# Norm rows spread by products with ones, and four places for rectified index scores

## The chip, the cores and the metric

The kernel runs on one core of one Trainium2 chip. The metric is the device time of one execution in microseconds (us). TensorE is called PE here, VectorE DVE, ScalarE ACT, GpSimd POOL and SyncE SP, as in the profile.

## The reference

A trunk of two layers for 1024 tokens of width 1024. Layer 0 mixes tokens with a gated short convolution, layer 1 with sparse attention: an indexer scores all earlier keys, the best 256 are kept, and attention runs over them. Each mixer and each mixture of experts is followed by a residual sum and a layer norm.

```python
for i in range(DEPTH):                       # 2 layers
    m = short_conv_mixer(x, ...) if i % 2 == 0 else dsa_mixer(x, ...)
    x = layer_norm(DEEPNORM_ALPHA * x + m, ln1_g[i], ln1_b[i])
    f = hier_moe(x, router_wg[i], ..., exp_w1[i], exp_w3[i], exp_w2[i])
    x = layer_norm(DEEPNORM_ALPHA * x + f, ln2_g[i], ln2_b[i])     # the second norm

def layer_norm(x, g, b):
    y = (x - mu) * rsqrt(var + LN_EPS) * g + b       # g and b: one row of 1024 for all tokens

# in dsa_mixer, for each block of 128 queries and 8 indexer heads of 64
s_idx = einsum('bthd,bsd->bths', q_idx, k_idx) * 64 ** -0.5
score = einsum('bths,bth->bts', relu(s_idx), w_idx)
```

The mixture has 8 groups of 8 experts of hidden width 256 (SwiGLU), two experts of one group for each token.

## The kernel before, in words

All work is written out in program order; each engine takes its own instructions in that order. SBUF holds an arena of 26 slots of 128 x 2048 f32. `take()` gives the slot that was freed longest ago, `give()` puts slots at the end of the list. An instruction that writes a slot waits until the last reader of its earlier contents is done.

`moe(l, ...)` goes over 32 pairs of experts, four pairs to a group of experts. For pair `p` it runs `up(p)` on PE (the products with both experts' first and third matrices, line 870, 64 instructions in column halves), `act(p)` (lines 878, 879), the sums of the pair before (`add`, line 922), `turn(p)` (line 885), at the last pair of a group `select()` for the next group (line 855), and `down(p)` (line 896). `down` makes two halves of 128 x 512; each half is read from PSUM by ACT (line 900), by DVE (line 901) and, up to pair 27, by ACT again (line 903). `select`, `turn` and `down` take their PSUM tiles in turn from the pool `psr`, which has three buffers; `up` has a buffer of its own. The expert matrices, 1 MB each, are loaded by SP (line 792) as soon as slots are free: `prefetch` is called behind every `give`. A pair uses six of them. `gather` and `scatter` on POOL bring and write rows of tokens; `finish` applies the second norm to a group's rows and first runs behind `down(4)`. Behind pair 6 `count_over` reads a number into registers, and the engines wait for it.

The second norm's scale and shift are needed in all 128 partitions. `load_ln` takes a slot behind pair 2 and loads each of the two rows with a DMA on ACT's queue that reads the same row for every partition (lines 161, 162).

In `attention()`, `index_queries(g)` makes the queries of two indexer heads on PE (lines 222 to 224, called `mm3`), ACT and DVE split them (1378, 1380), and SP swaps partition halves through `tm` (1383, 1384). One group later `scores(g)` is woven into the next `index_queries`: ACT first writes the swapped halves (1388, 1389); then, for each head and each of six blocks of queries, PE makes the scores in a PSUM tile of two banks (1401, 1402, pool `psL`, two buffers), ACT rectifies them into `r` (1405), and DVE adds `r` times the head's weight to the block's sum (1408 for the first head, 1410 for the others). `r` alternates between the two halves of one slot, `rl`. POOL splits the weights of the attention queries beside this (1423, 1424). The attention queries of 16 heads follow on PE, beside the search for the best keys on ACT and DVE.

Of the kernel before, what the change touches and what calls it, by code (L numbers as in the profile page):

```python
# [23 lines left out]
F32 = mybir.dt.float32  # L24
# [4 lines left out]
AF = mybir.ActivationFunctionType  # L29
# [4 lines left out]
P = 128  # L34
T = 1024
D = 1024
# [30 lines left out]
class Net:  # L67
# [32 lines left out]
    def constants(self):  # L100
        nc, c = self.nc, self.const
        sl = self.take()
        jp = self.slots[sl].bitcast(I32)[:, :P]
        nc.gpsimd.iota(jp, pattern=[[1, P]], base=0, channel_multiplier=-1)
        self.ident = c.tile([P, P], F32, name="ident")
        nc.vector.tensor_scalar(self.ident, jp, 0.0, None, op0=OP.is_equal)
        self.tri = c.tile([P, P], BF16, name="tri")
        nc.vector.tensor_scalar(self.tri, jp, 0.0, None, op0=OP.is_gt)
        self.ones = c.tile([P, P], BF16, name="ones")
        nc.vector.memset(self.ones, 1.0)  # L110
        self.io64 = c.tile([P, NE], F32, name="io64")
        nc.gpsimd.iota(self.io64, pattern=[[1, NE]], base=0, channel_multiplier=0,
                       allow_small_or_imprecise_dtypes=True)
        self.ioP = c.tile([P, NE], F32, name="ioP")
        nc.gpsimd.iota(self.ioP.rearrange("p (a b) -> p a b", a=2), pattern=[[1, 2], [2, NP]],
                       base=0, channel_multiplier=0, allow_small_or_imprecise_dtypes=True)
        self.tcol = c.tile([P, 1], F32, name="tcol")
        nc.gpsimd.iota(self.tcol, pattern=[[1, 1]], base=0, channel_multiplier=1,
                       allow_small_or_imprecise_dtypes=True)
        self.counts = c.tile([P, NC], F32, name="counts")  # L120
        self.nx = c.tile([P, 2], I32, name="nx")
        self.mhalf = c.tile([P, 1], F32, name="mhalf")
        nc.vector.memset(self.mhalf, -0.5)
        self.flip = c.tile([P, 1], I32, name="flip")
        nc.gpsimd.iota(self.flip, pattern=[[1, 1]], base=P - 1, channel_multiplier=-1)
        self.causal = c.tile([P, P], F32, name="causal")
        nc.vector.tensor_scalar(self.causal, jp, 0.0, FAR, op0=OP.is_gt, op1=OP.mult)
        self.give(sl)
        self.convk = c.tile([P, 3, KT], F32, name="convk")
        self.rows = c.tile([P, NB], I32, name="rows")  # L130
        self.rows0 = c.tile([P, NB], I32, name="rows0")
        self.codes = c.tile([P, 2, 2 * NG], F32, name="codes")
        self.first = c.tile([P, NB], F32, name="first")
        nc.vector.scalar_tensor_tensor(self.first, self.io64[:, :NB], float(NG), self.io64[:, :NB],
                                       op0=OP.is_lt, op1=OP.mult)
        nc.vector.tensor_scalar(self.first, self.first, float(2 * GP * CAP), None, op0=OP.mult)
        self.zero = c.tile([P, NG], F32, name="zero")
        nc.vector.memset(self.zero, 0.0)
        self.sgate = c.tile([P, NP], F32, name="sgate")
        self.srank = c.tile([P, NP], F32, name="srank")  # L140
        self.ovi = c.tile([P, NP], I32, name="ovi")
        self.sr7 = c.tile([P, GP], F32, name="sr7")
        self.jw = c.tile([P, 2], F32, name="jw")
        nc.gpsimd.iota(self.jw, pattern=[[P, 2]], base=P, channel_multiplier=0, allow_small_or_imprecise_dtypes=True)
        self.v6 = c.tile([P, NT, 6], F32, name="v6")
        nc.gpsimd.iota(self.v6, pattern=[[1, NT], [0, 6]], base=1, channel_multiplier=0,
                       allow_small_or_imprecise_dtypes=True)
        nc.gpsimd.tensor_copy(self.v6[:, :, 0], self.tcol.to_broadcast([P, NT]))
        self.gates = c.tile([P, NT, 2], F32, name="gates")
        self.xn = self.dram.tile([T, D], F32, name="xn")  # L150
        self.xres = self.dram.tile([T, D], F32, name="xres")
        self.Y = self.dram.tile([2 * T, D], F32, name="Y")
        self.Yov = [self.dram.tile([2 * P, D], F32, name=f"Yov{l}") for l in range(2)]
# [640 lines left out]
    def moe(self, l, out, last=None, split=None):  # L794
# [3 lines left out]
        nc, S, W = self.nc, self.slots, self.W  # L798
        R_ = lambda v: v.bitcast(F32R)
        mm = nc.tensor.matmul  # L800
        ctx = ExitStack()
        psh = ctx.enter_context(self.tc.tile_pool(name="ps_h", bufs=1, space=PSUM))
        psr = ctx.enter_context(self.tc.tile_pool(name="ps_r", bufs=3, space=PSUM))
# [200 lines left out]
        for p in range(NP):  # L1004
            g, i = divmod(p, GP)
            if p == NP - 1:
                residual_sums(0)
            ph = up(p)
            act(p, ph)
            places(p)  # L1010
            if p:
                add(p - 1, 0)
            turn(p)
            if p:
                add(p - 1, 1)
            if p == NP - 2:
                scale_rows()
            if i == GP - 1 and g + 1 < NG:
                select()
            down(p)  # L1020
            if g < NG - 1:
                beyond(p)
            if g and i == 0:
                for h in range(2):
                    residual(g - 1, h)
                finish(g - 1)
            if p < 2:
                gather(p + 1)
            if 0 < g < NG - 2 and i == 2:
                gather(g + 2)  # L1030
            if p == 2:
                self.load_ln(self.i["ln2_g"][l], self.i["ln2_b"][l], nc.scalar)
            if p == GP + 2:
                self.count_over()
            if i == GP - 2 and g + 1 < NG:
                parts(g + 1)
            if last and p == NP - 1:
                last()
            self.prefetch(l, 0)
            if p == NP - 2:  # L1040
                load_beyond()
# [232 lines left out]
    def attention(self):  # L1274
        nc, sm, mm = self.nc, self.small, self.nc.tensor.matmul
        w_in, w_out = self.i["attn_w_in"][0], self.i["attn_w_out"][0]
        S = self.slots
# [20 lines left out]
        kds = self.take()  # L1298
# [45 lines left out]
        for t in range(NT + 1):  # L1344
# [4 lines left out]
            if t >= 3:  # L1349
# [3 lines left out]
        xis = [self.take() for _ in range(2)]  # L1353
# [2 lines left out]
        sc2 = sm.tile([P, 384], F32, name="sc2", bufs=1)  # L1356
        sc = {7: S[scs[0]][:, :1024], 6: S[scs[0]][:, 1024:1920], 5: S[scs[1]][:, :768],
              4: S[scs[1]][:, 768:1408], 3: S[scs[1]][:, 1408:1920], 2: sc2}
        rl = self.take()
        blocks = (7, 6, 5, 4, 3, 2)  # L1360
        cnt = {"h": 0, "s": 0, "t": 0, "r": 0}

        def index_x(h):
            return S[xis[h // 2 % 2]][:, (h % 2) * T:(h % 2 + 1) * T]
# [21 lines left out]
        def scores(g):  # L1386
            tm = S[tms][:, (g % 2) * T:(g % 2 + 1) * T]
            nc.scalar.activation(R_(index_x(2 * g)[64:]), tm[64:], AF.Copy)
            nc.scalar.activation(R_(index_x(2 * g + 1)[:64]), tm[:64], AF.Copy)
            yield  # L1390
            for h in (2 * g, 2 * g + 1):
                x = index_x(h)
                for b in blocks:
                    n = (b + 1) * P
                    nch = 2 if n > 512 else 1
                    pt = psL.tile([P, 2, 512], F32, name="pL")
                    c = n // nch
                    for ch in range(nch):
                        ks = slice(ch * c, (ch + 1) * c)
                        q = R_(x[:, b * P:(b + 1) * P])  # L1400
                        mm(pt[:, ch, :c], q, R_(kdH[:, ks]), start=True, stop=False)
                        mm(pt[:, ch, :c], q, R_(kdL[:, ks]), start=False, stop=True)
                    r = S[rl][:, (cnt["s"] % 2) * T:(cnt["s"] % 2) * T + n]
                    cnt["s"] += 1
                    nc.scalar.activation(r.rearrange("p (a c) -> p a c", a=nch), pt[:, :nch, :c], AF.Relu)
                    w = wi[:, b, h:h + 1]
                    if h == 0:
                        nc.vector.tensor_scalar(sc[b], r, w, None, op0=OP.mult)
                    else:
                        nc.vector.scalar_tensor_tensor(sc[b], r, w, sc[b], op0=OP.mult, op1=OP.add)  # L1410
                    if h == IH - 1:
                        nc.vector.tensor_add(sc[b][:, n - P:], sc[b][:, n - P:], self.causal)
                    yield
# [294 lines left out]
        order = [(0, 0), (1, 0), (0, 1), (1, 1)] + [divmod(k, 2) for k in range(4, 2 * HEADS)]  # L1708
        for k, (h, hh) in enumerate(order):
            if k == 2:  # L1710
                self.give(kds, rl, *xis)
                open_q(4)
                js = self.take()
                jb, js_i = S[js].bitcast(BF16), S[js].bitcast(I32)[:, T:]
# [14 lines left out]
            s = wsl[h]  # L1729
            ts_ = slice(hh * 512, (hh + 1) * 512)  # L1730
            pt = ps.tile([P, 512], F32, name="pa")
# [155 lines left out]
        for t in range(NT):  # L1887
# [10 lines left out]
            else:  # L1898
                split_o(t + 1)
                for n in range(2):  # L1900
                    pt = new()
# [98 lines left out]
```

## Time and profile before

| what | us |
|---|---|
| median of 3 runs | 2241.94 (2241.01 to 2243.04) |
| profiled execution | 2247.03 |
| its span, first to last instruction | 2245.2 |
| PE busy in it | 2112.2 (94%) |
| DVE busy | 1164.9 (52%) |
| ACT busy | 846.4 (38%) |
| POOL busy | 398.9 (18%) |
| moved by DMA | 502.63 MB, mean 224 GB/s |

The profile is of one execution. The order of the stages in it: the convolution to about 280 us, its norm and routing to 415, the experts of layer 0 to 910, the scores of the indexer from 970 to 1060, the attention queries to 1220, attention and its output to 1720 with the routing, the experts of layer 1 to the end. Instructions of PE are pipelined, so that a busy PE isn't PE at its peak, and the busy share of the whole span is a mean over stages with different limits. An idle time is printed with what ended it: `[1.20 <-DMA slot<-in_exp_w_dram]` means 1.20 us of idleness that ended when that transfer landed.

### The profile page before, as it was taken

The page shows a single profiled execution, that of the slowest core. Times are in us where ns is not written, and L with a number is a line of the kernel's source. Part 1 is how long each engine was busy: PE and PEld are TensorE (multiplying, and loading weights), DVE is VectorE, ACT ScalarE, POOL GpSimd, SP SyncE. Part 2 cuts the span into 40 slices and gives each one's busy share as a digit, 9 for nine tenths or more (in the row PEclk, how much of TensorE's full clock was granted, in tenths as well). Part 3 has the DMA queues.
Part 4 walks back from the last instruction along what each step waited for, and adds up shares of the span by engine and source line. Part 5 has one row for each costly group of instructions (what it writes and reads, how often), then busy time and mean ns, then how long its engine had stood idle before and what let it go on. Part 6 is the DMA issues. An engine that isn't in the chain of part 4 may idle for free. (4 is left out here: it accounts for less than half of the span.)

```text
span 2245.2 us, 32773 instructions
## 1 busy us (share of the span) xinstructions
PE 2112.2 (94%) x12541; PEld 1542.4 (69%) x12541; DVE 1164.9 (52%) x2760; ACT 846.4 (38%) x1714; POOL 398.9 (18%) x477
## 2 busy tenths in 40 slices
PE   8999999798999999699999899999997999999997
PEld 7888888455555555577888789998886555555553
DVE  4333478432333333567786998773488233333333
ACT  3111211232333321356986877772211332333321
POOL 0000011110111110422332544321012011111100
PEclk9999999899999999899999999999998999999998
DMA  5113275599999999312112000003335799999995
GB/s 163 50 53 117 96 272 181 210 419 420 419 419 419 419 419 399 121 38 66 48 38 76 1 1 20 1 20 134 116 114 212 301 418 420 420 418 419 419 419 241
DMA packets 136778, 502.63 MB, mean 224 GB/s; under 512 B 23340, under 2 KB 69652, under 8 KB 86949
## 3 DMA queue, kind: packets, MB, share of 16 engines
q1 hardware_dynamic: 116608, 461.86, 52.2%
q0 software_dynamic: 16128, 32.09, 3.9%
q10 hardware_dynamic: 3876, 6.51, 0.8%
q8 instruction: 100, 1.64, 0.3%
q14 instruction: 66, 0.53, 0.1%
HBM read 476.70 MB, written 51.40 MB: 235 GB/s over the span
## 5 line engine op out<-in xcount | busy, mean ns | idle before, releaser
L870 PE MATMUL ph<-slot,slot 128*64 128x256 f32 x4096 | 462.1, 382 | 13.3 <-DVE nx L771 8.5
L870 PEld LDWEIGHTS ph<-slot,slot 128*64 128x64 f32 x4096 | 299.1, 138 | 192.2 <-issue 48.8
L901 DVE SCALAR_TENSOR_TENSOR slot<-rg,sgate,slot 128x512 fp32r<-128x512 f32 x128 | 96.1, 751 | 301.0 <-ACT slot L900 300.0
L896 PE MATMUL rg<-slot,slot 128*64 128x512 f32 x1024 | 234.2, 598 | 4.1 <-ACT slot L886 1.3
L210 ACT ACTIVATE slot<-slot 128x1024 fp32r<-128x1024 f32 (+2 forms) x151 | 119.0, 839 | 246.8 <-DVE slot L372 148.1
L222 PE MATMUL ps<-slot,slot 128*128 128x512 f32 x512 | 202.7, 396 | 1.1 <-DVE slot L211 0.8
L223 PE MATMUL ps<-slot,slot 128*128 128x512 f32 x512 | 199.5, 390 | 0.6 <-DVE slot L211 0.6
L224 PE MATMUL ps<-slot,slot 128*128 128x512 f32 x512 | 199.6, 390 | 0.0
L222 PE MATMUL po<-slot,slot 128*128 128x256 f32 (+1 forms) x544 | 189.3, 348 | 0.0
L931 POOL DMA_INDIRECT Yov<-slot,ovi x56 | 55.5, 992 | 728.2 <-ACT slot L903 728.2
L223 PE MATMUL po<-slot,slot 128*128 128x256 f32 (+1 forms) x544 | 181.2, 333 | 0.0
L224 PE MATMUL po<-slot,slot 128*128 128x256 f32 (+1 forms) x544 | 181.1, 333 | 0.0
L211 DVE TENSOR_TENSOR slot<-slot,slot 128x1024 fp32r<-128x1024 f32 (+2 forms) x146 | 125.3, 895 | 90.0 <-ACT slot L210 88.8
L896 PEld LDWEIGHTS rg<-slot,slot 128*64 128x64 f32 x1024 | 68.5, 136 | 139.1 <-issue 114.1
L879 DVE TENSOR_TENSOR slot<-slot,ph 128x256 f32<-128x256 f32 x64 | 26.9, 420 | 233.5 <-ACT slot L878 233.5
L222 PE MATMUL pa<-slot,slot 128*128 128x512 f32 (+1 forms) x384 | 144.4, 376 | 0.2 <-DVE slot L211 0.2
L223 PE MATMUL pa<-slot,slot 128*128 128x512 f32 (+1 forms) x384 | 143.2, 373 | 0.0
L224 PE MATMUL pa<-slot,slot 128*128 128x512 f32 (+1 forms) x384 | 143.2, 373 | 0.0
L900 ACT ACTIVATE slot<-rg,sgate 128x512 fp32r<-128x512 f32 x128 | 87.6, 684 | 133.8 <-PE rg L896 133.8
L855 PE MATMUL rg<-slot,slot 128*128 128x512 f32 x512 | 126.9, 405 | 5.2 <-ACT slot L210 3.1
L878 ACT ACTIVATE slot<-ph 128x256 f32<-128x256 f32 x64 | 24.6, 385 | 283.3 <-PE ph L870 283.3
L211 DVE TENSOR_TENSOR slot<-pT,slot 128x512 fp32r<-128x512 f32 (+1 forms) x160 | 101.0, 632 | 54.8 <-ACT slot L210 53.5
(319 smaller groups left out, 3870.1 us busy)
## 6 DMA issues: line engine op xcount, KB each, us to landing
slot<-in_exp_w_dram SPq DMA_DIRECT2D x380, 1024.0 KB
slot<-in_conv_w_in_dram SPq DMA_DIRECT2D x24, 512.0 KB
slot<-in_attn_w_in_dram SPq DMA_DIRECT2D x17, 512.0 KB
slot<-in_x_dram SPq DMA_DIRECT2D x16, 512.0 KB
slot<-xres SPq DMA_DIRECT2D x16, 512.0 KB
slot<-in_attn_w_out_dram SPq DMA_DIRECT2D x8, 1024.0 KB
xn<-slot POOLq DMA_DIRECT2D x14, 512.0 KB
slot<-in_conv_w_out_dram SPq DMA_DIRECT2D x8, 512.0 KB
```

The source lines that it names most:

```text
L210: self.nc.scalar.activation(hi.bitcast(F32R), raw, AF.Copy)
L211: (eng or self.nc.vector).tensor_sub(lo.bitcast(F32R), raw, hi)
L222: mm(out, ah.bitcast(F32R), bh.bitcast(F32R), start=start, stop=False)
L223: mm(out, ah.bitcast(F32R), bl.bitcast(F32R), start=False, stop=False)
L224: mm(out, al.bitcast(F32R), bh.bitcast(F32R), start=False, stop=stop)
L855: mm(pt, R_(S[xs[i]][:, j * D + k * P:j * D + (k + 1) * P]), R_(sel[i]), start=i == 0 and j == 0, stop=i == 1 and j == 1)
L870: mm(ph[q * CAP:(q + 1) * CAP, m * 256:(m + 1) * 256], gt[k][:, o + q * CAP:o + (q + 1) * CAP], w[:, k * 256:(k + 1) * 256], start=k == 0 ...
L879: nc.vector.tensor_mul(hg, hg, ph[:, 256:])
L896: mm(py[q * CAP:(q + 1) * CAP], hT[:, c * P + q * CAP:c * P + (q + 1) * CAP], w[:, c * D + n * 512:c * D + (n + 1) * 512], start=c == 0, s ...
L900: nc.scalar.activation(R_(hi), py, AF.Copy, scale=g)
L901: nc.vector.scalar_tensor_tensor(R_(lo), py, g, hi, op0=OP.mult, op1=OP.subtract)
L931: nc.gpsimd.indirect_dma_start(out=self.Yov[l][:, :], out_offset=bass.IndirectOffsetOnAxis(ap=self.ovi[:, p:p + 1], axis=0), in_=share(p), ...
```

## The change

Two parts. In `moe`, the slot of the norm is taken at the same place, behind pair 2, but each row is loaded once, 4 KB into one partition. Behind pair 3 four products of a column of ones (one row, 128 columns) with a quarter of the slot's first row spread it over 128 partitions in PSUM, in plain f32, in tiles of `psr`, and ACT copies each back over the slot. In `attention`, the rectified scores get two slots, and so four places.

```diff
@@ constants
+        self.one = c.tile([P, 1], F32, name="one")
+        nc.vector.memset(self.one, 1.0)
@@ moe, behind pair p
             if p == 2:
-                self.load_ln(self.i["ln2_g"][l], self.i["ln2_b"][l], nc.scalar)
+                self.ln_slot = self.take()
+                ln = S[self.ln_slot]
+                self.g_t, self.b_t = ln[:, :D], ln[:, D:]
+                for j, n in enumerate(("ln2_g", "ln2_b")):
+                    nc.scalar.dma_start(ln[0:1, j * D:(j + 1) * D], self.i[n][l:l + 1])
+            if p == 3:
+                for q in range(4):
+                    pt = psr.tile([P, 512], F32, name="rg")
+                    s = slice(q * 512, (q + 1) * 512)
+                    mm(pt, self.one[0:1].to_broadcast([1, P]), ln[0:1, s], start=True, stop=True)
+                    nc.scalar.activation(ln[:, s], pt, AF.Copy)
@@ attention
-        rl = self.take()
+        rls = [self.take() for _ in range(2)]
@@ scores
-                    r = S[rl][:, (cnt["s"] % 2) * T:(cnt["s"] % 2) * T + n]
+                    c4 = cnt["s"] % 4
+                    r = S[rls[c4 // 2]][:, (c4 % 2) * T:(c4 % 2) * T + n]
@@ behind the scores
-                self.give(kds, rl, *xis)
+                self.give(kds, *rls, *xis)
```

## Rows read from the trace of the kernel before

**Rows 1.** The page's slices, 40 equal parts of the span, busy tenths.
```profile
PE   8999999798999999699999899999997999999997
DMA  5113275599999999312112000003335799999995
```
**Rows 2.** Timeline of PE, end of layer 0's experts: start, us, line, count, idle before.
```profile
820.54 0.59 PE L870 MATMUL ph<-slot,slot 128*64 128x256 f32 x2
822.42 3.67 PE L870 MATMUL ph<-slot,slot 128*64 128x256 f32 x32 [1.28 <-DMA slot<-in_exp_w_dram]
827.39 3.67 PE L870 MATMUL ph<-slot,slot 128*64 128x256 f32 x30 [1.30 <-DMA slot<-in_exp_w_dram]
...
869.25 7.86 PE L870 MATMUL ph<-slot,slot 128*64 128x256 f32 x64
```
**Rows 3.** The same, end of layer 1's experts.
```profile
2148.10 4.05 PE L870 MATMUL ph<-slot,slot 128*64 128x256 f32 x34
2152.94 3.67 PE L870 MATMUL ph<-slot,slot 128*64 128x256 f32 x30 [0.80 <-DMA slot<-in_exp_w_dram]
...
2194.80 4.05 PE L870 MATMUL ph<-slot,slot 128*64 128x256 f32 x34
2200.05 3.67 PE L870 MATMUL ph<-slot,slot 128*64 128x256 f32 x30 [1.20 <-DMA slot<-in_exp_w_dram]
...
2211.51 7.66 PE L870 MATMUL ph<-slot,slot 128*64 128x256 f32 x64
```
**Rows 4.** SP's waits, first 490 to 600, then 700 to 860: us, times, longest.
```profile
SPq L792 <- PE ph L870: 40.4, 15, 6.0
...
SPq L792 <- DMA slot<-in_exp_w_dram: 137.0, 62, 3.5
```
**Rows 5.** DMA moved (packets, MB, share) and issued, 431 to 550, then 1757 to 1885.
```profile
q1 hardware_dynamic: 6104, 44.51, 91.2%
slot<-in_exp_w_dram SPq DMA_DIRECT2D x44, 1024.0 KB
...
q1 hardware_dynamic: 6568, 47.90, 91.0%
slot<-in_exp_w_dram SPq DMA_DIRECT2D x48, 1024.0 KB
```
**Rows 6.** ACT's DMA queue from 471 to 481: packets, MB, share of 16 engines.
```profile
q10 hardware_dynamic: 288, 1.05, 26.5%
```
**Rows 7.** Timeline behind down(3) of layer 0.
```profile
485.47 7.08 PE L870 MATMUL ph<-slot,slot 128*64 128x256 f32 x64
...
487.63 0.69 ACT L903 ACTIVATE slot<-rg,sgate 128x512 f32<-128x512 f32 x1 [0.82 <-DVE slot L901]
```
**Rows 8.** Timeline of PE, products of the residual with the identity.
```profile
882.99 1.98 PE L979 MATMUL pc<-slot,ident 128*128 128x512 f32 x4
```
**Rows 9.** PE's waits from 1003 to 1008.5, in the index scores.
```profile
PE pL L1401 <- ACT slot L1405: 2.6, 3, 1.4
```
**Rows 10.** Timeline of DVE, ACT and PE in the index scores.
```profile
1000.88 7.03 DVE L1410 SCALAR_TENSOR_TENSOR slot<-slot,wi,slot 128x896 f32<-128x896 f32 x4
...
1009.06 4.24 DVE L1410 SCALAR_TENSOR_TENSOR slot<-slot,wi,slot 128x1024 f32<-128x1024 f32 x4 [0.58 <-ACT slot L1405]
1013.50 1.41 DVE L1380 TENSOR_TENSOR slot<-pa,slot 64x512 f32<-64x512 f32 x2 [0.20 <-ACT slot L1378]
...
1017.56 1.06 ACT L1388 ACTIVATE slot<-slot 64x1024 fp32r<-64x1024 f32 x1 [3.09 <-DMA slot<-slot]
...
1018.67 0.50 PE L1401 MATMUL pL<-slot,slot 128*128 128x512 f32 x1 [0.17 <-ACT slot L1388]
```
**Rows 11.** The pair behind the register read; windows: us, PE, PEld, DVE, ACT, POOL busy, PEclk, DMA share, GB/s.
```profile
528.17 9.69 PE L870 MATMUL ph<-slot,slot 128*64 128x256 f32 x64 [4.36 <-DVE nx L771]
...
520.00:540.00 20.00, 15.29 (x89) 8.65 (x89) 7.91 (x21) 5.62 (x8) 2.02 (x2) 0.83 1.02 419
820.00:840.00 20.00, 17.15 (x107) 11.61 (x103) 9.12 (x13) 6.63 (x10) 1.02 (x1) 1.00 1.02 418
```

## The prediction

> **What bounds the kernel now.** I read the page's slices first. In slices 9 to 16 and 33 to 39 of 40 the transfer engines stand at 9 tenths, and TensorE (PE) at 9 in nearly all of them [rows 1]. So in both expert stages two resources are full at once, and the order in which they run out decides. The timeline of PE shows it. One pair of experts' up-projection is 64 products and takes 7.08 us when its weights are there [rows 7]. Late in the first stage one takes from 820.54 to 831.06, 10.52 us, with two idle times that end on an expert transfer, and the one at 869.25 takes 7.86 [rows 2]. The second stage has three late ones: 8.51 us from 2148.10, 8.92 from 2194.80, and 7.66 at 2211.51 [rows 3]. Against 7.08 that is 3.44 + 0.78 = 4.2 us of waiting for weights in the first stage and 1.43 + 1.84 + 0.58 = 3.85 in the second. The waits of SyncE's queue tell why they come late: from 490 to 600 it waits nearly always for PE to free a slot, from 700 to 860 for an earlier transfer [rows 4]. The stage begins on PE with a stock of loaded weights, PE eats the stock, and the last pairs run at the pace of the transfers. The stage of the index scores is another matter: PE is the bound, and the question there is which of its short idle times depend on the two places for rectified scores.
>
> **The change part by part: the norm's rows.** Removed: two 512 KB loads in each layer. In the ten microseconds from 471 their queue had 26.5% of all transfer time [rows 6], so 2.65 us of the transfers' time per layer. Two issues on ScalarE's queue remain two issues; the new ones move 4 KB each. SyncE's wait for the old load's landing goes; it was early, in the time in which SyncE mostly waits for PE, so I cost it at nothing.
>
> Added on PE, between down(3) and up(4): four products of one row with ones, 128x512 in plain f32, two instructions each. The nearest row is the residual's product with the identity, four instructions in 1.98 us [rows 8], 0.495 each, so 8 x 0.495 = 3.96 us. That row contracts 128 rows, the new one a single row. The bounds are therefore 0 (work added to a full engine is no gain) and 3.96; I take 3.96, because PE has no idle time there to hide them.
>
> Added waits: the four share PSUM pool psr (three buffers) with select, turn and down. The first takes the buffer of select's last part, which is free. The second takes that of down's first half, the third that of its second half, whose last reader is ScalarE's third copy, 487.63 + 0.69 = 488.32 [rows 7]. The first two products run from 485.47, where up(4) began, to 487.45; the third waits 0.87 us to 488.32; the fourth needs the first one's copy, which ScalarE makes behind that share, done before 489.31. So PE reaches up(4) 3.96 + 0.87 = 4.8 us later. Behind the wait on PE stand up(4) and the freeing of its slots, and with them SyncE's next expert loads. The four copies stand on ScalarE before act(4), in a time in which it had only waited for up(4), and cost nothing. The rows land before: the whole megabyte of the old loads, issued at the same place, was through by 481, and the first product starts at 485.47 [rows 6, 7], so 4.5 us are left even for loads as long as the old ones; if that cover were gone, the rest of the landing would be PE's wait. The slot is taken at the same place, and readers of the result, the first finish, come after up(4).
>
> What the delay is worth at the stage's end. PE's own path gets 4.8 later and sheds its waits: first stage 4.8 - 4.2 = +0.6, second 4.8 - 3.85 = +0.95. The transfers' path gets 2.65 earlier, but in the time in which SyncE waits for PE it can run dry when PE frees slots 4.8 later. Its stock: from 431 to 550, begun with an empty queue, 44 loads of 1.049 MB were issued, 46.1 MB, and 44.5 had moved; 1.6 MB, 4.0 us at the 1.05 MB in 2.65 us of [rows 6], were outstanding. In the second stage 48 loads, 50.3 MB, against 47.9: 2.4 MB, 5.9 us [rows 5]. The transfers are 2.65 ahead and the loads 4.8 late, 7.45 us together, so the first stage's engines stand still for 7.45 - 4.0 = 3.45 us and the second's for 1.55. Transfers' path: -2.65 + 3.45 = +0.8 and -2.65 + 1.55 = -1.1. The later path ends each stage: +0.8 and +0.95. The unknown is how much of that stock an issue's own delay eats: from none (as taken) to all of it, with which each stage would end 4.8 later; I take none, since the page shows no dry slice.
>
> **The change part by part: four places for scores.** ScalarE rectifies a PSUM tile into one of two places, VectorE (DVE) adds it up. The wait that this can remove is in one short stretch: from 1003 to 1008.5 PE waits three times for ScalarE, 2.6 us together [rows 9], while DVE is saturated, four additions in 7.03 us where the next four take 4.24 [rows 10]. With four places ScalarE runs on, and PE gains up to 2.6. But what comes due next? After these scores DVE subtracts the next queries (1013.50), a transfer swaps their halves, ScalarE writes them at 1017.56, and PE waits for that at 1018.67 [rows 10]. DVE starts that subtraction no sooner than it has finished its additions. Its idle time in the stretch is 0.58 before 1009.06 and 0.20 before 1013.50, so the chain comes about 0.7 us sooner and PE waits for the rest at its end. Bounds: 0, if DVE's additions lengthen, and -2.6, if PE keeps all of it; I take -0.7, by DVE's rows. From there to the end of the query projections PE's slices are full [rows 1], so it is passed on. The second slot costs no wait that I can find: takes go round a list of free slots, each moves up by one, and the four late query slots go to slots whose last readers are products and additions before the first copy into them. If that list were short, a POOL split or a load would wait. One column set to one at the start is hidden by the first loads.
>
> **Sum.** +0.8 + 0.95 - 0.7 = +1.05 us. The profiled execution took 2247.03 (span 2245.2, 1.8 around it), 5.1 above the median of 2241.94; against its own time that is 2248.1, on the median 2243.0.
>
> **The rivals.** (1) PE's clock falls at the products, slower. After the 4.36 us idle before up(7), 64 products took 9.69 us instead of 7.08, and the granted clock of 520 to 540 was 0.83, so part of it ran at 1.2 GHz and not 2.4; two idles of 1.3 us left it at 1.00 in 820 to 840 [rows 2, 11]. If the added stretch of one-row products and a wait acts like that idle, PE is 4.8 + 2.6 = 7.4 late: first stage -2.65 + 7.4 + 2.65 - 4.0 = +3.4, second 7.4 - 3.85 = +3.55, with -0.7 together +6.25, 2248.2. It decides where PE counts as idle. The Trainium skill, page TensorE: Matmul & The Clock Gate, section A second HAM failure mode: psum-queue depth-cycling, says that small idle times between groups of products that cycle through PSUM buffers can make the clock drop again and again; by that rule this rival would be the forecast, but the trace of before does not agree for idles of 1.3 us. (2) No stock: an empty queue costs the whole delay in both stages, 2 x 4.8 - 0.7 = +8.9, 2250.8; against it stands a transfer share of 9 tenths throughout. (3) The transfers alone end both stages: 2 x -2.65 - 0.7 = -6.0, 2235.9. It needs a stock over 7.45 us, and waits for weights over 7.45 us; the rows show 4.0 to 5.9 and 3.85 to 4.2. (4) PE keeps all 2.6 of the scores: -0.85, 2241.1. (5) The places are not what ScalarE waits for, and the scores give 0: 2243.7, inside the forecast.
>
> **How the numbers follow.** Forecast with (5) 0.58, (4) 0.16, clock 0.11, no stock 0.07, transfers alone 0.08. Two tenths of a percent, 4.5 us, is about what a measurement of this kernel can tell from no change: faster 0.08, same 0.74, slower 0.18. The range leaves out (2) and (3), 0.15: low, products near their lower bound or (4) with half the stall, 2239.0; high, the clock's case, 2248.2.
>
> **What would show it.** In each expert stage four products behind down(3), 0.9 to 1.0 us apart, with one wait of about 0.9; up(4) 4.8 later; the late up-projections at 7.1 us; some dry transfer time near 550; granted clock 1.00 after the products. In the scores, no wait of ScalarE for DVE and a longer wait before the third pair of heads. Wrong: late up-projections that stay late, a clock under 1.00 there, or scores that end 2 us earlier.

## The result and the profile after

The changed kernel took 2256.13 us (median of 4 runs, 2253.26 to 2257.26) against 2242.15: 1.0057 of the time before, interval 1.0044 to 1.0071, or 14 us slower. The forecast was 2243.0 and the range ended at 2248.2. The profiled execution took 2253.26, span 2251.4.

The timeline of PE behind down(3) of layer 0, where [rows 7] has only up(4) at 485.47, shows the added products, 1 row by 512 columns. The first two take 1.98 us, the second two 3.78, and up(4), now L872, takes 8.53 and not 7.08.

```profile
483.99 1.98 PE L1043 MATMUL rg<-slot,one 1*128 1x512 f32 x4
486.78 3.78 PE L1043 MATMUL rg<-slot,one 1*128 1x512 f32 x4 [0.81 <-ACT slot L905]
490.49 8.53 PE L872 MATMUL ph<-slot,slot 128*64 128x256 f32 x64
```

The windows of the same stretch say why (us, busy time of PE, PEld, DVE, ACT and POOL, then PEclk, DMA share, GB/s). The granted clock falls from 1.00 to 0.82 and 0.50, half being the lower level, 1.2 GHz. The fourth line, and the three of the wider windows under it, show the second loss: the transfers move 172 GB/s from 490 to 500, and 338 from 485 to 515, where the kernel before moved 420.

```profile
479.00:484.00 5.00, 5.00 (x24) 1.97 (x22) 1.44 (x2) 1.62 (x4) 0.00 (x0) 1.00 1.01 421
484.00:488.00 4.00, 3.19 (x8) 1.34 (x7) 0.75 (x1) 2.88 (x5) 0.98 (x1) 0.82 1.02 424
488.00:490.00 2.00, 2.00 (x3) 0.46 (x2) 0.00 (x0) 0.60 (x1) 0.00 (x0) 0.50 0.99 414
490.00:500.00 10.00, 9.69 (x68) 5.40 (x67) 0.49 (x2) 0.98 (x2) 0.00 (x0) 0.83 0.48 172
...
485.00:515.00 30.00, 27.96 (x169) 14.08 (x169) 8.59 (x14) 7.26 (x14) 4.93 (x5) 0.89 0.83 338
515.00:550.00 35.00, 29.98 (x192) 18.00 (x189) 11.62 (x28) 10.11 (x15) 2.98 (x3) 0.95 1.02 415
550.00:600.00 50.00, 48.40 (x341) 26.36 (x342) 17.49 (x28) 16.06 (x25) 8.00 (x8) 1.00 0.98 400
```

The same three windows of the kernel before:

```profile
485.00:515.00 30.00, 28.79 (x214) 15.75 (x212) 10.60 (x17) 8.77 (x15) 5.74 (x6) 1.00 1.02 420
515.00:550.00 35.00, 29.98 (x168) 17.86 (x166) 11.53 (x28) 9.35 (x14) 2.18 (x3) 0.90 1.01 419
550.00:600.00 50.00, 48.09 (x343) 27.15 (x340) 18.36 (x29) 15.37 (x25) 8.00 (x8) 1.00 1.02 420
```

Against 419 GB/s the changed kernel misses 81 x 30 + 4 x 35 + 19 x 50 = 3,520 KB, 8.4 us of transfer time: the **dry time**, which stands beside 2.65 us saved. At the stage's end PE still waits for expert transfers, as in [rows 2, 3], though less; in layer 0:

```profile
830.34 1.95 PE L872 MATMUL ph<-slot,slot 128*64 128x256 f32 x16 [0.64 <-DMA slot<-in_exp_w_dram]
...
876.45 3.67 PE L872 MATMUL ph<-slot,slot 128*64 128x256 f32 x30 [0.19 <-DMA slot<-in_exp_w_dram]
```

In the index scores the table of PE's waits from 1003 to 1020 (us, times, longest) has less waiting for rectified scores (L1418) and more for the swapped halves (L1400).

```profile
PE pL L1413 <- ACT slot L1400: 1.6, 1, 1.6
PE pL L1413 <- ACT slot L1418: 1.0, 2, 0.8
```

The same of the kernel before, L1405 being the rectified scores and L1388 the halves:

```profile
PE pL L1401 <- ACT slot L1405: 3.0, 4, 1.4
PE pL L1401 <- ACT slot L1388: 0.2, 1, 0.2
```

### The profile page after: what moved, and what is told of

Its sections match the earlier page's. It is cut to its first block, busy times and chain, and to the rows that moved or that the text cites. A ratio compares the mean times of both kernels' runs of the same rounds, so it can differ in the third digit from the quotient of the medians.

```text
span 2251.4 us, 32820 instructions
## 1 busy us (share of the span) xinstructions
PE 2121.4 (94%) x12557; PEld 1544.7 (69%) x12557; DVE 1165.0 (52%) x2761; ACT 850.6 (38%) x1722; POOL 398.9 (18%) x477
## 5 line engine op out<-in xcount | busy, mean ns | idle before, releaser
L872 PE MATMUL ph<-slot,slot 128*64 128x256 f32 x4096 | 462.8, 383 | 10.3 <-DVE nx L773 8.6
L872 PEld LDWEIGHTS ph<-slot,slot 128*64 128x64 f32 x4096 | 300.1, 138 | 190.7 <-issue 51.1
```

Of the source, the lines that this page charges most:

```text
L872: mm(ph[q * CAP:(q + 1) * CAP, m * 256:(m + 1) * 256], gt[k][:, o + q * CAP:o + (q + 1) * CAP], w[:, k * 256:(k + 1) * 256], start=k == 0 ...
```

## The experiments

**One table for all.** From the timeline of PE I read where the up-projections of pair 0 and pair 8 start and where that of pair 31 ends. "Late" is how much later than before pair 8 starts, "longer" how much later pair 31 ends, both counted from pair 0. The two kernels with an untouched norm, before and scores_alone, are the base (pair 8 at 122.42 and 121.52, the end at 463.97 and 463.14 in layer 0; ends at 463.51 and 462.95 in layer 1; means used). "Dry" is worked out for layer 0 as above, from windows at the same times, with none missing where a window moved 419 or more; "saved" is what the loads of the kernel leave out. Time is against the median of before beside it (2242.2 to 2242.8), with the ratio's interval.

| kernel | late, L0 | dry - saved | longer, L0 | longer, L1 | time |
|---|---|---|---|---|---|
| after, first trace | 7.4 | 8.4 - 2.65 = 5.8 | 5.1 | 6.1 | +14.0 (1.0044-1.0071) |
| after_again | 9.8 | 10.6 - 2.65 = 8.0 | 7.4 | 8.6 | +12.9 (1.0037-1.0068) |
| norm_alone | 7.7 | 8.5 - 2.65 = 5.9 | 5.3 | 6.2 | +15.7 (1.0048-1.0079) |
| loads_row1 | 7.7 | 5.6 - 0 = 5.6 | 5.6 | 6.0 | +17.3 (1.0061-1.0092) |
| loads_row128 | 5.7 | 3.6 - 0 = 3.6 | 3.6 | 4.0 | +8.1 (1.0023-1.0050) |
| rows32 | 6.1 | 5.7 - 2.0 = 3.7 | 3.9 | 2.6 | +9.1 (1.0031-1.0061) |
| products_ahead | 6.5 | 7.1 - 2.65 = 4.4 | 4.5 | 5.0 | +11.1 (1.0037-1.0068) |
| rows_full | 9.7 | 10.0 - 2.65 = 7.4 | 7.7 | 8.6 | +18.2 (1.0065-1.0096) |
| pool_spread | 10.4 | 10.8 - 2.65 = 8.1 | 7.8 | 8.5 | +17.8 (1.0068-1.0096) |
| no_rows | 0.1 | 1.1 - 2.65 = -1.5 | -2.2 | -0.8 | -3.2 (0.9973-0.9992) |
| pool_early | 0.2 | 1.2 - 2.65 = -1.4 | -1.6 | -1.4 | -2.1 (0.9982-1.0000) |
| pool_early_scores | -0.1 | 1.1 - 2.65 = -1.5 | -2.5 | 2.3 | -4.5 (0.9971-0.9991) |

In layer 0 dry minus saved agrees with the lengthening to within 0.7 us in all but the last, and to 1.0 there. The same windows counted from pair 0 of layer 1 agree to within 0.8 (dry there: 8.6 in the first trace of the change, 3.6 in loads_row128). So the transfers' account ends the stage, and what sets it is how late PE frees slots.

**Which part made the loss: norm_alone and scores_alone.** norm_alone is the change without its three places in the scores, scores_alone those alone, of which two are:

```
-        rl = self.take()
+        rls = [self.take() for _ in range(2)]
...
-                    r = S[rl][:, (cnt["s"] % 2) * T:(cnt["s"] % 2) * T + n]
+                    c4 = cnt["s"] % 4
+                    r = S[rls[c4 // 2]][:, (c4 % 2) * T:(c4 % 2) * T + n]
```

> The norm part alone: rows loaded and spread by products, the scores with their two places as before. Theory (the clock falls at the one-row products): the first products 0.5 us each, the later ones 0.87, up(4) 8.5 us instead of 7.08 in both expert stages, PE about 8 us late behind them, and a time 10 to 16 us above the kernel before. Rival A (the delay of PE alone, clock unchanged: products 3.96 plus a wait of 0.8): up(4) 7.1 us, time +2 to +6. Rival B (the scores' part, or the slots that it shifts, made the loss): time within 4 us of before.

> The four places in two slots alone, the norm's rows loaded as before. Theory: the scores end 0.7 to 1.7 us sooner on PE, as in the trace of after, and nothing else moves: 2240 to 2242 us, no more than 2.6 us below before. Rival B (the extra slot held over the stage delays other takes, or its gain is paid back): 4 us or more above before, with new waits of DMA issues or of PE for slots between 1000 and 1500 us.

scores_alone took 2241.04, ratio 0.9996, interval 0.9987 to 1.0005: it fits the -0.7 forecast, and neither 0 nor -2.6 is excluded. norm_alone took 2258.25. The loss is the norm's.

**Rows contracted, all else equal: loads_row1 and loads_row128.** Both keep the old loads and put four products on top. They differ in the rows that a product contracts (and in the column's value, 1/128 for 128 rows):

```
+                    mm(pt, self.one[0:1].to_broadcast([1, P]), ln[0:1, s], start=True, stop=True)
...
+                    mm(pt, self.one.to_broadcast([P, P]), ln[:, s], start=True, stop=True)
```

> The two loads that spread the norm's rows stay as before (1 MB per layer), and the four one-row products with their copies are added on top, at the same place, writing the same values over them. It takes the saved transfers out of the norm part, and nothing else. Theory (transfers are late behind the delayed PE, so their bytes count): 2 x 2.65 = 5.3 us above the norm part alone, less where the engines run dry anyway; bound 0. If it equals the norm part alone, the saved megabyte per layer is worth nothing. up(4) 8.5 us as there.

> As the one before, with the same loads, the same number of products, copies, buffers and waits, but each product contracts all 128 rows (with 1/128 in place of ones, so the values stay). Theory (one-row products do not count as work for the clock): products stay at 0.5 us, up(4) at 7.1 us, granted clock 1.00 around them, PE 4.8 us late instead of 8 and the time 5 to 8 us below the run with one-row products. Rival A (rows do not matter; the wait for ScalarE or the plain f32 products themselves bring the clock down, or it is the delay alone): the same time within 2 us and the same up(4) as there.

loads_row1 took 2259.90 and loads_row128 2250.72, 9.2 us apart (5 to 8 expected) with the same loads, buffers and waits. Timeline of PE in loads_row1:

```profile
487.94 2.85 PE L1040 MATMUL rg<-slot,one 1*128 1x512 f32 x4 [0.81 <-ACT slot L905]
490.72 9.58 PE L872 MATMUL ph<-slot,slot 128*64 128x256 f32 x64
```

And in loads_row128, with its window from 488 to 490 in a fence of its own:

```profile
488.47 1.98 PE L1040 MATMUL rg<-slot,one 128*128 128x512 f32 x4 [0.81 <-ACT slot L905]
490.38 7.13 PE L872 MATMUL ph<-slot,slot 128*64 128x256 f32 x64
```

```profile
488.00:490.00 2.00, 1.53 (x4) 0.68 (x4) 0.00 (x0) 1.76 (x4) 0.99 (x1) 1.00 0.99 414
```

With full rows the clock holds at 1.00 through the same wait; in loads_row1 the same window has 0.73. The delay by itself still cost 8.1 us. And loads_row1 against norm_alone prices the saved megabytes behind a late PE: 1.65 us by the medians, with overlapping intervals, and +0.2 and -0.2 us in the two stages. They are spent as dry time.

**Does the wait matter, and how many rows are enough: products_ahead and rows32.** products_ahead moves the four one-row products ahead of down(3), where their buffers are free. rows32 loads each row into 32 partitions and contracts those. Of products_ahead the place, of rows32 the load and the product (its column holds 1/32):

```
             select()
+            if p == 3:
+                for q in range(4):
...
             down(p)
```

```
+                    nc.scalar.dma_start(ln[0:32, j * D:(j + 1) * D], self.bcast(self.i[n][l], D)[0:32])
...
+                    mm(pt, self.one[0:32].to_broadcast([32, P]), ln[0:32, s], start=True, stop=True)
```

> The norm part alone with its four one-row products moved ahead of the down-projection of the pair, 3.6 us earlier, so that their PSUM buffers are free and PE does not stand still between them. Theory (the one-row products by themselves bring the clock down): the work behind them runs at half speed for some microseconds all the same, and only the wait of 0.8 is saved: 2256 to 2258. Rival (the idle of 0.8 us between products of one row is what lets the clock fall): products 0.5 us each, the down-projection behind at 3.65 and up(4) at 7.1, PE 4.0 late, 2249 to 2251.

> As the norm part alone, but each row is loaded into 32 partitions (256 KB per layer) and the products contract 32 rows with 1/32 in place of ones. Theory (the granted clock falls where a product uses few of the array's rows): if 32 rows are enough, products at 0.5 us, up(4) 7.1 us and about 2250 us as with 128; if they are too few, products that grow to 0.87, up(4) 8.5 to 9.6 and about 2257. Rival (the clock fell by the wait, and 128 rows only happened to escape): 2257 as well, with 0.5 us for the products ahead of the wait and slow ones after it.

products_ahead took 2253.87, 2 below the theory's range, rows32 2251.87. Timeline of PE in products_ahead:

```profile
479.49 4.45 PE L1026 MATMUL rg<-slot,one 1*128 1x512 f32 x8
483.87 6.24 PE L898 MATMUL rg<-slot,slot 128*64 128x512 f32 x16
```

The same view of rows32, in layer 0 and in layer 1:

```profile
488.77 8.81 PE L872 MATMUL ph<-slot,slot 128*64 128x256 f32 x64
...
1819.68 7.13 PE L872 MATMUL ph<-slot,slot 128*64 128x256 f32 x64
```

Without any idle between them, the one-row products still bring the clock down: the down-projection behind them takes 6.24 us where the kernel before has 3.65 (granted clock 0.50 in the window from 484 to 488). So the wait isn't needed for the fall. With 32 rows the clock fell in layer 0 (8.81) and held in layer 1 (7.13), in one and the same execution. The expectations had 32 rows as enough or too few; they are neither.

**Full rows and the saving together: rows_full.** POOL sets the slot to zero ahead of the two row loads, and the products contract 128 rows, 127 of them zero:

```
+                nc.gpsimd.memset(ln, 0.0)
                 for j, n in enumerate(("ln2_g", "ln2_b")):
                     nc.scalar.dma_start(ln[0:1, j * D:(j + 1) * D], self.i[n][l:l + 1])
...
+                    mm(pt, self.one.to_broadcast([P, P]), ln[:, s], start=True, stop=True)
```

> The norm part alone with products over all 128 rows: POOL sets the slot to zero, the two rows are loaded into its first partition as in the change, and the products contract 128 rows, of which 127 are zero. The megabyte stays saved. Theory (full rows keep the clock; the saved transfers are lost while the engines wait for slots that PE frees late): products 0.5 us, up(4) 7.1, and with PE 4.9 late and the transfers 2.65 early the same end as the run that loads all and contracts 128 rows, 2249 to 2251. Rival (the saved transfers count once the clock holds): 5.3 us below that run, 2244 to 2246. If up(4) is at 8.5 or more, rows of zeros do not count as work, and the time is near 2257.

It took 2260.98, which no theory had. The timelines of ACT, POOL and PE show that the kernel brought a delay of its own:

```profile
469.07 1.83 POOL L1037 MEMSET slot<- 128x2048 f32 x1
470.93 0.26 ACTq L1039 DMA_DIRECT2D slot<-in_ln_g_dram  x1
471.59 2.12 ACT L212 ACTIVATE slot<-slot 128x1024 fp32r<-128x1024 f32 x1 [3.85 <-DMA slot<-in_ln_g_dram]
476.12 0.51 PE L887 MATMUL rg<-ident,slot 128*128 128x128 f32 x2 [3.48 <-DVE slot L881]
492.29 1.98 PE L1044 MATMUL rg<-slot,one 128*128 128x512 f32 x4 [0.81 <-ACT slot L905]
494.20 7.13 PE L872 MATMUL ph<-slot,slot 128*64 128x256 f32 x64
```

ACT's row loads wait on its queue for POOL's zeros until 470.93; behind them ACT's split and activation of pair 3 come late, and PE stands 3.48 us. It answers two things all the same. Rows of zeros hold the clock (1.98 and 7.13). And PE late by 9.7 us costs as much with the clock up: its stages, 7.7 and 8.6 longer, are those of after_again, 7.4 and 8.6. (The two profiled executions are still 4.2 us apart, of which the stretch between the two stages has 2.8; rows_full has the two places for scores, after_again four.) What it can't answer is whether the saving would have counted at a delay of 4.8.

**The rows without PE: no_rows, pool_spread and pool_early.** no_rows leaves the norm's scale and shift out (ones and zeros by POOL). pool_spread has one broadcast over partitions by POOL where the products stood; pool_early issues it a pair sooner, with one tiny operation behind it. In place of the loads in no_rows, then behind the row loads in pool_early:

```
+                nc.gpsimd.memset(self.g_t, 1.0)
+                nc.gpsimd.memset(self.b_t, 0.0)
...
+                nc.gpsimd.partition_broadcast(ln, ln[0:1])
+                nc.gpsimd.tensor_scalar(self.pz, self.mhalf, 1.0, None, op0=OP.mult)
```

> The norm's rows are not loaded at all: POOL sets the scale to one and the shift to zero, so the second norm's scale and shift are left out of what is computed. It is the value of the saved megabyte by itself. Theory: as with the broadcast on POOL, 2237 to 2239. Rival: 2241 to 2243. If this one is faster and the broadcast is not, the broadcast itself costs.

> The norm's rows loaded as one row, as in the change, but spread by one broadcast over partitions on POOL at the same place, with nothing added on PE or ScalarE; the scores as before. Theory (the transfers end both expert stages, and the delay of PE made their engines run dry): no dry transfer time beyond that of before, the stage 2 to 2.65 us shorter in each layer, 2237 to 2239 us. Rival (the saved megabyte is worth nothing, as the run with both loads and products suggests, where it cost 1.6 us at most): 2241 to 2243. Rival (the POOL work delays its own gathers): above 2243.

> The broadcast on POOL issued a pair earlier, right behind the row loads, where POOL has 18.6 us without work, with one tiny POOL operation behind it, so that the two standstills of 8 to 9 us that stood around the broadcast end before the first norm's steps on POOL; the scores as before. Theory (those standstills made the 17.8 us): no wait of the first norm for POOL, PE as in the kernel before, the stage 1 to 2 us shorter per layer as without rows, 2239 to 2240. Rival (the broadcast slows something else in that stretch, or the standstill comes back later): 2250 or more, with a wait for POOL in the trace.

no_rows took 2239.59, 3.2 below before and just above what the theory gave: the saved megabytes do pay while PE is on time. By the median it is less than 2 x 2.65, which the interval (1.8 to 6.1 us) doesn't exclude; the trace has 1.1 us of dry time, with transfers that run ahead. pool_spread took 2260.59. Timelines of POOL, DVE and PE:

```profile
497.61 2.31 POOL L1038 PARTITION_BROADCAST slot<-slot  x1 [8.22 <-issue]
511.28 0.25 POOL L233 TENSOR_SCALAR st<-st 128x1 f32<-128x1 f32 x1 [9.09 <-issue]
512.25 1.28 DVE L245 SCALAR_TENSOR_TENSOR slot<-slot,st,slot 128x1024 f32<-128x1024 f32 x1 [8.27 <-POOL st L234]
513.92 0.70 PE L885 MATMUL rg<-ident,slot 128*128 128x128 f32 x2 [8.33 <-DVE slot L879]
```

The broadcast takes 2.31 us, but POOL stands 8.22 us ahead of it and 9.09 ahead of its next ordinary operation, which is the first norm's; DVE waits for that, and PE for DVE. A MODIFY_POOL_CONFIG instruction starts each standstill, at 489.4 and at 502.3; the kernel before has none there. In the view of the broadcast's line:

```profile
L1038 POOLq MODIFY_POOL_CONFIG  x4: 44/56/68, 489.4 to 1821.3; - x4
```

In pool_early both standstills fall ahead of the first norm, and PE's wait there is 0.87 us in layer 0, where the kernel before has 0.78: 2240.69, with an interval that reaches 1.0000. Its POOL timeline:

```profile
479.26 2.30 POOL L1038 PARTITION_BROADCAST slot<-slot  x1 [9.90 <-PE rg L856]
491.59 0.26 POOL L1039 TENSOR_SCALAR pz<-mhalf 128x1 f32<-128x1 f32 x1 [10.03 <-issue]
```

**Both parts in a form that pays: pool_early_scores.**

> As pool_early, with the four places for scores in two slots. Theory: the two gains add, 3 us of the saved megabyte and 1.5 of the scores: 2237 to 2239 us, below the kernel before and the change. Rival (the broadcast still costs): 2248 or more.

2238.31 us, ratio 0.9981, interval 0.9971 to 0.9991: 4.5 us below the kernel before and some 17 below the change. In its trace the gain is in layer 0. Layer 1's stage was 2.3 longer in that execution, because POOL came late to the first norm: its second standstill took 10.46 us, and the indirect write behind that, from 1822.76, kept it until 1824.72. Timelines of DVE and PE:

```profile
1825.67 1.28 DVE L246 SCALAR_TENSOR_TENSOR slot<-slot,st,slot 128x1024 f32<-128x1024 f32 x1 [1.86 <-POOL st L235]
1827.34 0.50 PE L886 MATMUL rg<-ident,slot 128*128 128x128 f32 x2 [1.92 <-DVE slot L880]
1828.38 5.31 PE L897 MATMUL rg<-slot,slot 128*64 128x512 f32 x16
```

DVE waited 1.86 us for POOL and PE 1.92 for DVE; the down-projection behind took 5.31 for 3.65, at a granted clock of 0.72 from 1828 to 1834. In layer 0, and in both layers of pool_early, DVE's wait was 0.49 to 0.81, and the kernel before has 0.78. So the place for the standstills is right only by a few microseconds, and one of the four layers seen missed it.

**The spread between executions: after_again.**

> The changed kernel once more, unaltered, for the spread between executions. Theory (its clock falls differ in length from one execution to the next): up(4) between 8.5 and 9.6 us in each layer and stages of 468.5 to 470 us, 2254 to 2258. Rival (something outside the expert stages adds the part of the loss that the stages of the first trace do not show, 3 to 4 us): stages as in the first trace and a longer stretch between them.

2255.70, as the first time. Timeline of PE in layer 0 and layer 1:

```profile
486.34 3.77 PE L1043 MATMUL rg<-slot,one 1*128 1x512 f32 x4 [0.81 <-ACT slot L905]
490.05 10.12 PE L872 MATMUL ph<-slot,slot 128*64 128x256 f32 x64
...
1821.42 10.03 PE L872 MATMUL ph<-slot,slot 128*64 128x256 f32 x64
```

up(4) took 10.12 and 10.03 here, above the 9.6 expected at most, and 8.53 and 8.98 in the first trace. The stages came to +7.4 and +8.6 against +5.1 and +6.1, 4.8 us more, and the profiled execution took 2256.58 against 2253.26. The length of the slow stretch varies, and with it the time. That can account for the first trace's stages, +11.2, showing less than the 14 us measured: its execution was the fastest of the four. That loads_row1 shows +11.6 in its stages and +17.3 in its median goes the same way (its profiled execution was its fastest, 2256.46), but 2 us of it stay unexplained.

## Why the prediction was wrong

**PE's delay: the step that failed first.** The form of the products was right: 0.495 each at full clock, a wait of 0.81 for 0.87. But the products of one row were priced by a row with 128 [rows 8], and the text took up(4) as 7.08. Measured by the starts of successive up-projections, PE was in layer 0 6.6 late at up(4) and 8.0 behind it in the first trace, 9.6 behind it in the second, for 4.8. Rival (1) had the mechanism, with 7.4; I gave it 0.11 because two idles of 1.3 us had left the clock at 1.00 [rows 11]. That row speaks of idles, and the fall needs none (products_ahead). The rule of the Trainium skill, page TensorE: Matmul & The Clock Gate, section A second HAM failure mode: psum-queue depth-cycling, that small idle times between groups of products cycling through PSUM buffers drop the clock, is not what was at work: the same cycling through buffers with full rows held the clock (loads_row128).

**The stock: the term that was mis-sized most.** The sum would leave 4.8 - 4.0 = 0.8 us dry for a delay of 4.8 with all loads kept. loads_row128 is just that kernel and had 3.6, of which 3.3 lie in this one window:

```profile
550.00:560.00 10.00, 10.00 (x67) 5.65 (x67) 2.66 (x4) 3.83 (x6) 1.00 (x1) 1.00 0.75 279
```

In layer 1, with a stock of 5.9 (6.1 by the text's own division), none was forecast and 3.6 came too. Issued less moved is a right count of what is outstanding, but it was taken at 550 and 1885, and the stock is lowest just ahead of the next loads, which the kernel before issues at 550.68 and, in layer 1, at 1878.29. The same view of the kernel before, first 431 to 550.6, then 1757 to 1878.2:

```profile
q1 hardware_dynamic: 6140, 44.77, 91.2%
slot<-in_exp_w_dram SPq DMA_DIRECT2D x44, 1024.0 KB
...
q1 hardware_dynamic: 6181, 45.08, 90.4%
slot<-in_exp_w_dram SPq DMA_DIRECT2D x44, 1024.0 KB
```

Of 46.14 MB issued, 1.37 and 1.06 MB are outstanding there, 3.3 and 2.5 us at 419 GB/s. And a queue that has run empty doesn't start at full pace. Behind its first dry stretch the changed kernel issues again at 495.59 (timeline of SP); its windows:

```profile
495.59 4.26 SPq L794 DMA_DIRECT2D slot<-in_exp_w_dram  x4
...
496.00:497.00 1.00, 1.00 (x12) 0.66 (x10) 0.00 (x0) 0.00 (x0) 0.00 (x0) 1.00 0.81 106
497.00:498.00 1.00, 1.00 (x14) 0.62 (x12) 0.00 (x0) 0.00 (x0) 0.00 (x0) 1.00 0.50 197
498.00:499.00 1.00, 1.00 (x11) 0.47 (x7) 0.00 (x0) 0.00 (x0) 0.00 (x0) 1.00 1.06 451
```

In the 2.4 us to 498 it moves 0.3 MB, 0.7 us of transfers: 1.7 us are lost (by the same working 1.5 at the stage's first loads in the kernel before, issued at 431.76). So of the 4.0 us of stock in layer 0, 3.3 - 1.7 = 1.6 was there, and of the 5.9 in layer 1 0.8. In loads_row128 pair 8 starts 5.3 us later than in this trace of before, and 5.3 - 1.6 = 3.7 for 3.6 dry. The text's own form, saved + late - stock, with 1.6 for the stock and "late" against this trace (0.45 less than in the table), comes within 0.6 us of the dry time in each of the twelve rows. It is worked out from the traces; no run tried the stock by itself. It also says where the saved megabytes go: transfers that are 2.65 ahead leave 2.65 less outstanding, and run dry as much longer.

The text named this unknown ("how much of that stock an issue's own delay eats") and took none of it, because the page of before shows no dry slice. That was no evidence: a kernel on time hides how near the edge it is. Rival (2), no stock, was nearer; with rival (1) on top, which I had priced as if apart, both came.

**What PE gets back at the end.** The late up-projections were to shed 4.2 and 3.85 us of waits. In the first trace PE came 7.4 late into the first layer's rest and 5.1 late out of it, so 2.3 was shed, since the transfers had become late too.

**What held.** The saved loads, the scores' -0.7 (waits for places 3.0 to 1.0, given back in part at the swapped halves, 0.2 to 1.6: -0.6 on PE), the copies on ACT, the rows landing in time and the slots all went as written. SP's waits for PE grew from the 40.4 of [rows 4] to 48.3, and the late ones for transfers stayed, 136.3 for 137.0.

Put together by the measured terms, two stages of +5.1 to +7.4 and +6.1 to +8.6 with -0.6 are +10.6 to +15.4, around the 13 to 14 measured. By loads_row128 some 8 us of it are PE's work and wait alone, and the rest is the clock. (loads_row128 keeps the old loads; that the saving would be lost at full clock too follows from the sum above, and no run shows it.)

## What to carry to other kernels

Where two resources are full, what is outstanding at one moment is not slack. To price a delay on the one that feeds the other, count the stock at its lowest point behind the delay, take off what an empty queue loses at its restart, and count saved transfers against it. A product of few rows is not a small product: it takes the time of a full one and can slow the work behind it, so a broadcast by products belongs where PE isn't the bound; full rows spare the clock, not the delay. A spare engine can do it for less, if its own standstills are placed where nobody waits, with room to spare.

## What the runs showed of the hardware

- The granted clock of PE fell to 0.50 behind products of one row with no idle between them (products_ahead), held at 1.00 with 128 rows, even with 127 of them zero (loads_row128, rows_full: 1.98 and 7.13), and with 32 rows fell once and held once.
- Behind an idle of 0.81 us PE's clock held with full rows (loads_row128); behind one of 1.92 us it was 0.72 (pool_early_scores, layer 1).
- Expert loads issued onto an empty queue moved 106 and 197 GB/s in the first two whole microseconds and 451 in the third (changed kernel).
- POOL's broadcast over partitions took 2.3 us in each of six places, with 7.9 to 9.9 us of idle time ahead of it and 9.1 to 10.5 ahead of the next ordinary operation, each with a MODIFY_POOL_CONFIG at its start. The Trainium skill, page GPSIMD Engine Reference, section 2.1 Instruction dispatch, says that the first call of a freshly loaded kernel pays a load of about 6 us more. The trace has more, 8.2 us from that instruction to the broadcast and 9.0 to the next operation in pool_spread, and has it twice.
